# Rotation pieces, half buffers, small clears and a norm's scaled sum in a two-layer diffusion step

## The chip, the cores and the metric

The kernel runs on one core of a Trainium2 chip. The metric is the device time of one launch in microseconds; the median of the runs is compared. TensorE does the matrix products, VectorE (DVE in the rows) and ScalarE (ACT) the elementwise work, GpSimd (POOL) elementwise work and its own DMA queue, and SyncE (SP) issues most loads.

## The reference, cut to what matters

One inference step of a backbone of width 1024 over 128 context and 512 latent tokens (640 in all), two layers. Layer 0 is attention: queries and keys are normed per head,

```
q = rms_norm(qkv[:, :, 0], q_gain); k = rms_norm(qkv[:, :, 1], k_gain)
rms_norm(x, g) = x * rsqrt(mean(x * x) + EPS) * g
```

context tokens attend to one another, latent tokens to a two-dimensional neighbourhood and to 256 cached context keys. Layer 1 is a diagonal complex state-space mixer in two directions: 64 groups of 16 channels, 64 states each, `x[t] = a x[t-1] + B u[t]`, `y = Re(C x) + D u`, then GELU and a gated linear map. Each layer is followed by a SwiGLU FFN of width 2816; every part begins with an RMS norm, modulated by a shift and a scale that come from the conditioning.

## The kernel before, in words

Activations lie with features on the partitions and the 640 tokens along the free dimension, in two halves of 320. A float32 product is made of three products of rounded parts: a matrix is split into a high part (ScalarE copies it) and a low part (VectorE or Pool subtracts).

The stages in order are `attention_layer`, `attention_out`, `ffn`, `ssm_layer`, `glu` and `fast_ffn`. TensorE's order in attention is written out by hand; on the other engines a planner that simulates the timeline orders the instructions, by program order and its own estimate of when each is ready. `issue_after` holds instructions back until a given one has been placed.

**Attention.** `start` norms the input and projects queries and keys of the first pair of heads. `projections` does the other eleven jobs (seven of queries and keys, four of values); each job has three groups of token tiles (two, two and one). A group of queries and keys goes through `qk_norm`: ScalarE squares, VectorE sums per head (L578), Pool forms the mean plus epsilon (L580) and its power of -0.5 (L581), VectorE scales (L588, tile `yn`). Eight steps later `qk_store` transposes the result on TensorE (L606, tile `tq`). A group of values goes through `v_split`. Between those steps run 80 attention units (`scores`, `weigh`, `values`), one for each pair of heads, query block and head.

**Rotations.** The state-space layer needs tables of powers of a complex number (`rotations`, one call for each of eight feature tiles). Pool computes them in the background of attention: doublings by L1180 to L1182, copies by L1189 to L1193 and a store to memory. `rotations` is a generator of nine pieces for each tile, 72 in all, that `self.turns` yields. `qk_norm` takes two or three pieces each time, and the loop of units one piece for each of the last 32 units (L405). In `start` the list is empty.

**Preparation of the state-space matrices.** `ssm_prep` is a generator too, taken step by step within `attention_out` and `ffn`. After its first part it goes through 16 steps (a feature tile and a half of it). A step loads the next step's chunk (`cb`, two buffers) and inputs (`qb`, two buffers), forms the chunk outputs (`co`, one buffer, stored to `cd`), then by a complex product `cmul` the input matrices (`bout`, one buffer for real and imaginary part, stored to `bd`), then the chunk response (`td` in memory, copied to `md`). All these loads and stores go through Pool's queue.

**State-space layer.** `ssm_tables` loads the tables of one feature tile; that of tile 0 is called within `ffn`. `states` calls it for the others and loads the response matrix `mt` by itself. Before the loop Pool clears `xb` (5200 columns) and both `w` (657 columns each). `ssm_input`, just before, norms the FFN's output into `u`, sends it to `uu` through SP's and Pool's queues, and takes the sums of squares of the last feature tiles.

Of the kernel before, what the change touches and what calls it, by code (L numbers as in the profile page):

```python
# [11 lines left out]
F32 = mybir.dt.float32  # L12
# [5 lines left out]
ALU = mybir.AluOpType  # L18
# [4 lines left out]
P = 128  # L23
D = 1024
KT = D // P
# [3 lines left out]
HEADS = 16  # L29
HD = 64  # L30
# [4 lines left out]
EPS = 1e-6  # L35
# [3 lines left out]
GC = 16  # L39
TC = 8  # L40
GT = P // GC
NST = 64
NCOL = 81
WROW = 82
# [55 lines left out]
class Kernel:  # L100
# [240 lines left out]
    def attention_layer(self, x0):  # L341
        tc, nc, a = self.tc, self.nc, self.a
        with ExitStack() as es:
# [10 lines left out]
                jobs += [("qk", 2 * c), ("v", c), ("qk", 2 * c + 1)]  # L354
            self.jobs = iter(jobs)
            self.jw, self.jqk, self.jv = [], {}, {}
            self.turns = iter(())
            with tc.manual_schedule(engines={nc.tensor.engine}):
                self.start(x0, es)
            ot = self.xp.tile([P, NPAIR, NTOK], F32, tag="x", name="ot")  # L360
            fill = itertools.chain(self.projections(len(jobs) - 1), self.out_start(ot))
            ada = iter([(wh, ft) for wh in (GA, 4, 3) for ft in range(KT)])
            self.ed = self.dp.tile([KT, P, 2, GT, NCOL], F32, name="ed")
            self.turns = itertools.chain(*(self.rotations(ct) for ct in range(KT)))
            units = [(hp, b, j) for hp in range(NPAIR) for b in range(-1, 4) for j in range(2)]
            n = len(units)

# [5 lines left out]
            with tc.manual_schedule(engines={nc.tensor.engine}):  # L373
                while at < PRE - JOB:
                    next(fill)
                    at += 1
                    if at == -JOB + FA:
                        self.qk_store(self.first[0][0], 0, 2, 0)
                    if at == -JOB + FB:
                        for t, y in enumerate(self.first[1]):  # L380
                            self.qk_store(y, 2 + 2 * t, 2 - t, 0)
                for i in range(-4, n + 1):
                    to = (PRE - JOB) * (-1 - i) // 4 if i < 0 else goal[min(i + 1, len(goal) - 1)]
                    if i + 4 < n:
                        st[i + 4] = self.scores(*units[i + 4])
                    half = at + (to - at) // 2
                    while at < half:
                        next(fill, None)
                        at += 1
                    if 0 <= i + 2 < n:  # L390
                        self.weigh(st[i + 2])
                    if i > 0 and units[i - 1][2]:
                        self.turn(st[i - 1], ot)
                        if i % 10 == 0:
                            self.turned.append(i // 10 - 1)
                    while at < to:
                        next(fill, None)
                        at += 1
                    if 0 <= i < n:
                        self.values(st[i], st.get(i - 1))  # L400
                    if i >= 0 and i % 10 in (3,6,9):
                        w = next(ada, None)
                        if w:
                            self.later(*w, 0)
                    if i >= n - 2 * HEADS:  # L405
                        next(self.turns, None)
                for _ in fill:
                    pass
                for _ in self.turns:
                    pass  # L410
                self.out_split(ot)
# [155 lines left out]
    def qk_norm(self, parts):  # L567

        nc = self.nc
        v = lambda ap: ap.rearrange("p (t d) -> p t d", d=HD)  # L570
        ss = self.ap.tile([P, 12], F32, tag="ss", name="ss", bufs=4)
        sums, g = [], 0
        for ps in parts:
            n = ps.shape[1]
# [2 lines left out]
            sums.append(ss[:, g : g + n // HD])  # L577
            nc.vector.tensor_reduce(sums[-1], v(sq), axis=AX.X, op=ALU.add)  # L578
            g += n // HD
        nc.gpsimd.tensor_scalar(ss[:, :g], ss[:, :g], 1.0 / HD, EPS, op0=ALU.mult, op1=ALU.add)  # L580
        last = nc.gpsimd.tensor_tensor(ss[:, :g], ss[:, :g], self.mhalf[:, :g], op=ALU.pow)  # L581
        ys, c = [], 512
        for ps, r in zip(parts, sums):
# [5 lines left out]
            c += n  # L589

        with self.tc.issue_after(last.ins):
            for _ in range(2 if n > 256 else 3):
                next(self.turns, None)
        return ys

# [28 lines left out]

    def v_split(self, c, ps, t0, n):
        nc = self.nc
        if t0 == 0:
            y = self.ap.tile([P, 2 * P], F32, tag="rr", name="vnew")
            nc.scalar.activation(y, ps[:, 0].rearrange("p h d -> p (h d)"), AF.Copy)
            nc.sync.dma_start(self.o["new_v"][:, c * 2 * P : (c + 1) * 2 * P], y)  # L630
        for pr in range(2):
            vp = self.jv[2 * c + pr]
            self.v_parts(lambda i: vp[:, i, t0 : t0 + n, :], ps[:, :, pr, :])
# [454 lines left out]
    def ssm_prep(self):  # L1088
# [56 lines left out]
        steps = [(ct, h) for ct in range(KT) for h in range(2)]  # L1145
        cb, qb, copies, before = self.load_chunk(0, 0), self.load_inputs(0, 0, qd), [], None
        for n, (ct, h) in enumerate(steps):
            ahead = n + 1 < len(steps) and (self.load_chunk(*steps[n + 1]), self.load_inputs(*steps[n + 1], qd))
            c = self.chunk_outputs(ct, h, pt, fe, cb)
            yield  # L1150
            self.input_matrices(ct, h, qb)
            cb, qb = ahead or (None, None)
            yield
            if copies:
                copies.pop()()
            if before:
                copies.append(self.chunk_response(*before, dcol))
                yield
            before = ct, h, c
        copies.pop()()  # L1160
        self.chunk_response(*before, dcol)()

    def rotations(self, ct):

# [42 lines left out]
    def input_matrices(self, ct, h, qb):  # L1207

        nc, sp = self.nc, self.sp
        n = 8 * NST  # L1210
        o = sp.tile([P, 2, n], F32, tag="o", name="bout")
        tmp = sp.tile([P, n], F32, tag="tmp", name="btmp")
        self.cmul(nc.vector, o[:, 0, :], o[:, 1, :], qb[:, 0, 0, :], qb[:, 0, 1, :], qb[:, 1, 0, :], qb[:, 1, 1, :], tmp)
        nc.gpsimd.dma_start(self.bd[ct, :, :, 4 * h : 4 * h + 4, :].rearrange("p i g l -> p i (g l)"), o)

    def load_chunk(self, ct, h):

        cb = self.sp.tile([P, 2, 2, 4, GC], F32, tag="cb", name="cb", bufs=2)
        self.nc.gpsimd.dma_start(cb.rearrange("p a i g c -> p (a i g c)"), self.a["ssm_cb"][2 * ct + h])
        return cb  # L1220

# [35 lines left out]
    def chunk_response(self, ct, h, c, dcol):  # L1257
# [7 lines left out]
            dm[64:], self.ident[64:MR, 64:MR].unsqueeze(1).broadcast_to([GC, n, GC]),  # L1265
            dcol[64:, gs : gs + n].unsqueeze(2).broadcast_to([GC, n, GC]), op=ALU.mult,
        )
        td = self.dp.tile([GC, n, (2 * TC - 1) * GC], F32, tag="td", name="td", bufs=2)
        kk = sp.tile([MR, n, LS * GC], F32, tag="kk", name="kk")
        ps = self.aux.tile([P, 512], F32, tag="aux", name="kkps")  # L1270
        with self.tc.issue_after(self.done.ins), self.tc.high_priority(offset=-LOW):
# [46 lines left out]
    def ssm_tables(self, ct):  # L1318
# [6 lines left out]
        cm = [(self.mp if ct % 2 else self.tables).tile([P, 2, GT // 2, P], F32, tag="cm", name="cm", bufs=2) for _ in range(2)]  # L1325
        for h in range(2):
            nc.sync.dma_start(cm[h], self.cd[ct, h])
        return bt, et, cm

    def ssm_layer(self):  # L1330
        tc, nc, a = self.tc, self.nc, self.a
# [4 lines left out]
        with self.ssm as es:  # L1336
# [13 lines left out]
            nc.gpsimd.memset(dmask[:, LC + 1 : LC + 2], 0.0)  # L1350
            w = [rp.tile([P, NW + 1], F32, name=f"w{i}") for i in range(2)]
            xb = rp.tile([P, 8 * NX + 16], F32, name="xb")
            nc.gpsimd.memset(xb, 0.0)
            dc = rp.tile([P, NW + 1], F32, name="dec")
            nc.gpsimd.memset(dc[:, NW:], 0.0)
            for i in range(2):
                nc.gpsimd.memset(w[i], 0.0)
            self.z, zt = self.htiles(True)
            def states(ct):

                tab = self.tab.pop(ct) if ct in self.tab else self.ssm_tables(ct)
                mt = [mp.tile([P, GT // 2, P], F32, tag="mt", name="mt", bufs=3) for _ in range(2)]
                for h in range(2):
                    self.loaded = nc.sync.dma_start(mt[h], self.md[ct, h])
                ps = []
                for i in range(2):
                    s = psa.tile([P, 2, 512], F32, tag=f"s{i}", name="sps")
# [241 lines left out]
```

## Time and profile before

| | |
|---|---|
| median of 3 runs | 1746.0 us (1740.94 to 1749.78) |
| profiled execution, its own time | 1747.1 us |
| its span | 1745.3 us |
| TensorE, weight loads | 1628.6 us (93%), 1564.8 us (90%) |
| VectorE | 1358.8 us (78%) |
| ScalarE | 698.7 us (40%) |
| Pool | 569.7 us (33%) |
| mean granted TensorE clock | 0.961 |

The span runs from the first to the last instruction of one profiled execution. Busy time of an engine leaves out its waits; an engine that is 93% busy has little left to give, but an average hides stretches in which it waits or runs at a lower granted clock. Attention ends near 440 us, the output map near 500, the first FFN near 1030, the state-space layer near 1180.

### The profile page before, as it was taken

To read this page: it belongs to the slowest core of one execution; us is meant where nothing else is said; L and a number is where in the kernel's file an instruction comes from. 1 tells how busy PE (TensorE), PEld (TensorE's weight loads), DVE (VectorE), ACT (ScalarE), POOL (GpSimd) and SP (SyncE) were. 2 spreads that over 40 slices of the span, in tenths; PEclk is the share of its full clock that TensorE was granted. 3 is DMA by queue.
4 is the path that set the end of the run, shared out by engine and by line. 5 is a ranking of instruction groups with operands and counts; after the bars stand their busy time and mean duration, and the time that the engine had idled before them with its cause. 6 is when DMAs were issued, how large, how long until landed. Compare 5 with 4: busy or idle time off the path is not lost.

```text
span 1745.3 us, 31855 instructions
## 1 busy us (share of the span) xinstructions
PE 1628.6 (93%) x12172; PEld 1564.8 (90%) x12172; DVE 1358.8 (78%) x2812; ACT 698.7 (40%) x1616; POOL 569.7 (33%) x848
## 2 busy tenths in 40 slices
PE   7999999988989989998899967989999899999999
PEld 1899899877979989998799967979999899999999
DVE  7677778786897778977896667986789975994793
ACT  4555555564554221322322233333245432551450
POOL 1155454976411322332230012240005612531430
PEclk9899999996999989999899987989999999999999
DMA  9233323343445676777677317856421131222222
GB/s 356 78 103 107 125 100 117 103 137 109 118 118 171 191 203 187 229 205 187 182 218 256 108 33 195 252 157 223 155 97 49 67 103 59 87 97 73 73 80 79
DMA packets 93369, 243.86 MB, mean 140 GB/s; under 512 B 24544, under 2 KB 34336, under 8 KB 92064
## 3 DMA queue, kind: packets, MB, share of 16 engines
q1 hardware_dynamic: 71520, 194.02, 34.0%
q0 software_dynamic: 21696, 47.80, 10.7%
q8 instruction: 96, 1.57, 0.4%
q14 instruction: 57, 0.47, 0.1%
HBM read 209.04 MB, written 31.52 MB: 138 GB/s over the span
## 4 chain that ended last, share of the span: by engine, by line
PE 68%; DVE 18%; DMA 6%; issue 3%; POOL 3%; ACT 2%; SPq 0%; DVEq 0%; POOLq 0%; ACTq 0%
PE p L166 27%; PE qkps L530 8%; PE fz L914 3%; PE pg L166 3%; PE pv L166 3%; DMA bd<-bout 3%; PE mmps L166 3%; DVE adaj L198 2%; PE po L706 2%; PE fy L914 2%; PE s L668 2%; PE fx L914 2%; PE fv L914 2%; PE fw L914 2%; PE s L670 2%
## 5 line engine op out<-in xcount | busy, mean ns | idle before, releaser
L166 PE MATMUL p<-bt,wh 128*128 128x320 f32 x1408 | 322.3, 316 | 13.8 <-DVE silu L814 7.4
L166 PEld LDWEIGHTS p<-bt,wh 128*128 128x128 f32 x1408 | 241.0, 192 | 16.6 <-DVE bt L241 6.7
L166 PE MATMUL p<-hh,wh 128*128 128x320 f32 x704 | 221.9, 316 | 13.1 <-ACT hh L244 12.3
L166 PE MATMUL p<-hh,wl 128*128 128x320 f32 x704 | 221.4, 315 | 4.6 <-DVE wl L114 4.6
L166 PE MATMUL p<-bt,wl 128*128 128x320 f32 x704 | 221.2, 315 | 0.8 <-DVE wl L114 0.7
L166 PE MATMUL p<-hl,wh 128*128 128x320 f32 x704 | 221.3, 315 | 0.7 <-DVE hl L245 0.7
L198 DVE SCALAR_TENSOR_TENSOR adaj<-adaw,cs 128x1024 bf16<-128x1024 f32 x160 | 197.1, 1232 | 0.3
L909 POOL TENSOR_TENSOR wsum<-wraw 128x512 f32<-128x512 f32 x90 | 125.9, 1400 | 206.3 <-DVE wl L245 145.0
L530 PE MATMUL qkps<-wh,hh 128*128 128x256 f32 x480 | 152.5, 318 | 0.0
L166 PEld LDWEIGHTS p<-hh,wh 128*128 128x128 f32 x704 | 134.7, 191 | 14.3 <-ACT hh L244 13.1
L113 ACT ACTIVATE wh<-wraw 128x1024 fp32r<-128x1024 f32 (+1 forms) x100 | 103.9, 1040 | 100.5 <-DMA wraw<-in_w 48.1
L166 PEld LDWEIGHTS p<-hh,wl 128*128 128x128 f32 x704 | 134.7, 191 | 5.1 <-DVE wl L114 5.1
L114 DVE TENSOR_TENSOR wl<-wraw,wh 128x1024 fp32r<-128x1024 f32 (+1 forms) x98 | 120.2, 1228 | 23.9 <-ACT wh L113 22.9
L530 PE MATMUL qkps<-wh,hl 128*128 128x256 f32 x480 | 137.5, 286 | 0.8 <-DVE hl L241 0.8
L530 PE MATMUL qkps<-wl,hh 128*128 128x256 f32 x480 | 137.4, 286 | 0.0
L166 PEld LDWEIGHTS p<-bt,wl 128*128 128x128 f32 x704 | 134.8, 192 | 1.4 <-DVE wl L114 1.4
L166 PEld LDWEIGHTS p<-hl,wh 128*128 128x128 f32 x704 | 134.4, 191 | 1.5 <-DVE hl L245 1.3
L245 DVE TENSOR_TENSOR wl<-wraw,wh 128x512 fp32r<-128x512 f32 (+1 forms) x128 | 103.2, 815 | 28.2 <-ACT wh L244 28.0
L251 DVE SCALAR_TENSOR_TENSOR ot<-p,mod,ot 128x64 f32<-128x64 f32 x192 | 64.5, 381 | 67.2 <-PE p L166 67.1
L244 ACT ACTIVATE wh<-wraw 128x512 fp32r<-128x512 f32 (+1 forms) x128 | 76.1, 611 | 83.1 <-PE p L166 57.3
L245 DVE TENSOR_TENSOR wl<-wsum,wh 128x512 fp32r<-128x512 f32 x90 | 92.7, 1030 | 15.0 <-ACT wh L244 14.5
L530 PEld LDWEIGHTS qkps<-wh,hh 128*128 128x128 f32 x480 | 93.0, 194 | 9.5 <-issue 1.5
(381 smaller groups left out, 4450.5 us busy)
## 6 DMA issues: line engine op xcount, KB each, us to landing
adaw<-in_ada SPq DMA_DIRECT2D x80, 512.0 KB, 3.9
wraw<-in_w SPq DMA_DIRECT2D x60, 512.0 KB, 4.6
wraw<-in_w SPq DMA_DIRECT2D x30, 1024.0 KB, 5.0
wraw<-in_w_qk SPq DMA_DIRECT2D x16, 512.0 KB, 3.8
qb<-in_ssm_bc POOLq DMA_DIRECT2D x16, 512.0 KB, 10.1
qb<-qd POOLq DMA_DIRECT2D x16, 512.0 KB, 8.4
cd<-co POOLq DMA_DIRECT2D x16, 512.0 KB, 8.4
bd<-bout POOLq DMA_DIRECT2D x16, 512.0 KB, 11.1
```

What stands on the lines that cost most here:

```text
L113: nc.scalar.activation(wh[:, :nk, :], raw[:, :nk, :], AF.Copy)
L114: (eng or nc.vector).tensor_tensor(wl[:, :nk, :], raw[:, :nk, :], wh[:, :nk, :], op=ALU.subtract)
L166: self.done = self.nc.tensor.matmul(ps, w[x][k // 4][:, k % 4, :] if isinstance(w[x], list) else w[x][:, k, :], h[y][k][:, c0 : c0 + HALF] ...
L198: nc.vector.scalar_tensor_tensor(junk, raw, 1.0, self.cs[:, cond, :], op0=ALU.mult, op1=ALU.mult, accum_out=self.macc[:, layer, which, ft, ...
L244: self.nc.scalar.activation(hi, x, AF.Copy)
L245: self.mark = self.nc.vector.tensor_tensor(lo, x, hi, op=ALU.subtract)
L251: self.mark = nc.vector.scalar_tensor_tensor(xi, pi, self.modcol(layer, gate_which, m, c), xi, op0=ALU.mult, op1=ALU.add)
L530: self.nc.tensor.matmul(ps, self.h[x][k][:, t * P : (t + 1) * P], w[y][k // 4][:, k % 4, :], start=(k == 0 and i == 0), stop=(k == KT - 1 ...
L668: nc.tensor.matmul(s[:, PAST:], qk[x][rows, 0, qc : qc + P], c[y][rows, :], start=(i == 0), stop=(i == 2))
L670: nc.tensor.matmul(s[:, :n], qk[x][rows, 0, qc : qc + P], qk[y][rows, 1, kc : kc + n], start=(i == 0), stop=(i == 2))
L909: nc.gpsimd.tensor_tensor(v, q[:, x], q[:, y], op=op)
L914: nc.tensor.matmul(ps[n], w[x][:, k * P : (k + 1) * P], b[right][y][:, k, :], start=(k == 0 and i == 0), stop=(k == 3 and i == 2))
```

## The change

- `self.ed` and `self.turns` are made before `start`, so that its two norms take pieces too. Every norm takes two pieces, every `v_split` takes two (with nothing that holds them back), and the loop of units none.
- In `qk_norm` the scaled sum is formed by VectorE; the power stays on Pool.
- In `ssm_prep` the next chunk is loaded after the present chunk's outputs are formed, into one buffer in place of two. `input_matrices` writes real and imaginary part to tiles of half the size, with three buffers, and stores each by a DMA of its own. The response's tile in memory has three buffers in place of two, and its copy to `md` is issued a step later.
- `ssm_tables` loads `mt` too, from a pool that is open during the FFN.
- Of `xb` only the first 16 columns of rows 1 to 7 and the last 16 are cleared, of each `w` only nine columns.

```diff
@@ attention_layer
+            self.ed = self.dp.tile([KT, P, 2, GT, NCOL], F32, name="ed")
+            self.turns = itertools.chain(*(self.rotations(ct) for ct in range(KT)))
-            self.turns = iter(())
             with tc.manual_schedule(engines={nc.tensor.engine}):
                 self.start(x0, es)
...
-            self.ed = self.dp.tile([KT, P, 2, GT, NCOL], F32, name="ed")
-            self.turns = itertools.chain(*(self.rotations(ct) for ct in range(KT)))
...
-                    if i >= n - 2 * HEADS:
-                        next(self.turns, None)
@@ qk_norm
-        nc.gpsimd.tensor_scalar(ss[:, :g], ss[:, :g], 1.0 / HD, EPS, op0=ALU.mult, op1=ALU.add)
+        nc.vector.tensor_scalar(ss[:, :g], ss[:, :g], 1.0 / HD, EPS, op0=ALU.mult, op1=ALU.add)
         last = nc.gpsimd.tensor_tensor(ss[:, :g], ss[:, :g], self.mhalf[:, :g], op=ALU.pow)
...
         with self.tc.issue_after(last.ins):
-            for _ in range(2 if n > 256 else 3):
+            for _ in range(2):
                 next(self.turns, None)
@@ v_split
+        for _ in range(2):
+            next(self.turns, None)
@@ ssm_prep
-            ahead = n + 1 < len(steps) and (self.load_chunk(*steps[n + 1]), self.load_inputs(*steps[n + 1], qd))
+            more = n + 1 < len(steps)
+            ahead = self.load_inputs(*steps[n + 1], qd) if more else None
             c = self.chunk_outputs(ct, h, pt, fe, cb)
+            cb = self.load_chunk(*steps[n + 1]) if more else None
             yield
             self.input_matrices(ct, h, qb)
-            cb, qb = ahead or (None, None)
+            qb = ahead
             yield
-            if copies:
-                copies.pop()()
+            if len(copies) > 1:
+                copies.pop(0)()
...
-        copies.pop()()
-        self.chunk_response(*before, dcol)()
+        copies.append(self.chunk_response(*before, dcol))
+        for c in copies:
+            c()
@@ input_matrices
-        o = sp.tile([P, 2, n], F32, tag="o", name="bout")
+        o = [sp.tile([P, n], F32, tag="o", name="bout", bufs=3) for _ in range(2)]
...
-        nc.gpsimd.dma_start(self.bd[ct, :, :, 4 * h : 4 * h + 4, :].rearrange("p i g l -> p i (g l)"), o)
+        for i in range(2):
+            nc.gpsimd.dma_start(self.bd[ct, :, i, 4 * h : 4 * h + 4, :].rearrange("p g l -> p (g l)"), o[i])
@@ load_chunk
-        cb = self.sp.tile([P, 2, 2, 4, GC], F32, tag="cb", name="cb", bufs=2)
+        cb = self.sp.tile([P, 2, 2, 4, GC], F32, tag="cb", name="cb")
@@ chunk_response
-        td = self.dp.tile([GC, n, (2 * TC - 1) * GC], F32, tag="td", name="td", bufs=2)
+        td = self.dp.tile([GC, n, (2 * TC - 1) * GC], F32, tag="td", name="td", bufs=3)
@@ ssm_tables
-        return bt, et, cm
+        mt = [self.tables.tile([P, GT // 2, P], F32, tag="mt", name="mt", bufs=3) for _ in range(2)]
+        for h in range(2):
+            self.loaded = nc.sync.dma_start(mt[h], self.md[ct, h])
+        return bt, et, cm, mt
@@ ssm_layer
-            nc.gpsimd.memset(xb, 0.0)
+            nc.gpsimd.memset(xb[:, NX : 8 * NX].rearrange("p (r c) -> p r c", c=NX)[:, :, :16], 0.0)
+            nc.gpsimd.memset(xb[:, 8 * NX :], 0.0)
...
-                nc.gpsimd.memset(w[i], 0.0)
+                nc.gpsimd.memset(w[i][:, 0 : NW + 1 : WROW], 0.0)
...
-                tab = self.tab.pop(ct) if ct in self.tab else self.ssm_tables(ct)
-                mt = [mp.tile([P, GT // 2, P], F32, tag="mt", name="mt", bufs=3) for _ in range(2)]
-                for h in range(2):
-                    self.loaded = nc.sync.dma_start(mt[h], self.md[ct, h])
+                *tab, mt = self.tab.pop(ct) if ct in self.tab else self.ssm_tables(ct)
```

## Rows read from the trace of the kernel before

**Rows 1.** The page: busy us, share of the span, instructions.

```profile
PE 1628.6 (93%) x12172; PEld 1564.8 (90%) x12172; DVE 1358.8 (78%) x2812; ACT 698.7 (40%) x1616; POOL 569.7 (33%) x848
```

**Rows 2.** Busy time by stretch: its length, engines, granted clock, DMA share, GB/s.

```profile
core 0: us, PE busy (x) PEld busy (x) DVE busy (x) ACT busy (x) POOL busy (x), PEclk, DMA share, GB/s
70.00:92.00 22.00, 22.00 (x95) 19.76 (x96) 11.58 (x33) 10.34 (x26) 0.00 (x0) 0.53 0.14 49
380.00:400.00 20.00, 8.04 (x70) 7.00 (x69) 12.51 (x24) 9.85 (x21) 19.19 (x25) 0.62 0.67 217
400.00:420.00 20.00, 19.50 (x138) 16.95 (x136) 13.13 (x35) 8.11 (x26) 18.44 (x49) 0.53 0.31 104
520.00:870.00 350.00, 323.43 (x2177) 320.58 (x2178) 276.22 (x546) 106.50 (x208) 97.64 (x139) 0.95 0.70 196
```

**Rows 3.** Waits of TensorE, 60 to 440 us: total, times, longest.

```profile
PE tq L606 <- DVE yn L588: 23.4, 11, 6.1
```

**Rows 4.** Timeline of Pool in attention: start, duration, instruction.

```profile
381.33 0.65 POOL L580 TENSOR_SCALAR ss<-ss 128x8 f32<-128x8 f32 x1
382.06 2.04 POOL L732 TENSOR_TENSOR hl<-ot,hh 128x640 fp32r<-128x640 f32 x1
...
386.21 1.64 POOL L581 TENSOR_TENSOR ss<-ss,mhalf 128x8 f32<-128x8 f32 x1
```

**Rows 5.** Timeline of TensorE there; in brackets the idle time before.

```profile
388.64 1.11 PE L606 MATMUL tq<-ident,yn 128*128 128x128 f32 x4 [6.11 <-DVE yn L588]
...
398.75 0.66 PE L606 MATMUL tq<-ident,yn 128*128 128x128 f32 x2 [5.85 <-DVE yn L588]
```

**Rows 6.** Waits of TensorE, 520 to 870 us.

```profile
PE p L166 <- ACT hh L244: 10.4, 2, 5.9
PE p L166 <- DVE silu L814: 7.4, 2, 4.8
```

**Rows 7.** Waits of VectorE, 500 to 870 us.

```profile
DVE bout L1014 <- DMA bd<-bout: 56.8, 12, 6.7
...
DVE co L1014 <- DMA cd<-co: 2.7, 2, 1.6
```

**Rows 8.** Timeline of Pool in one step of the preparation: its issues.

```profile
608.72 0.62 POOL L1204 DMA_DIRECT2D qb<-in_ssm_bc  x1
609.31 0.76 POOL L1214 DMA_DIRECT2D bd<-bout  x1
616.35 0.88 POOL L1234 DMA_DIRECT2D cd<-co  x1 [6.28 <-DVE co L1022]
```

**Rows 9.** Timeline of VectorE in that step.

```profile
605.29 0.68 DVE L1016 TENSOR_TENSOR bout<-bout,btmp 128x512 f32<-128x512 f32 x1
...
623.14 0.69 DVE L1014 TENSOR_TENSOR bout<-qb 128x512 f32<-128x512 f32 x1 [6.67 <-DMA bd<-bout]
...
629.53 0.76 DVE L1014 TENSOR_TENSOR co<-ptab,cb 128x576 f32<-128x576 f32 x1
```

**Rows 10.** DMA issues by line: count, size, median us to landing.

```profile
cd<-co POOLq DMA_DIRECT2D x16, 512.0 KB, 8.4
bd<-bout POOLq DMA_DIRECT2D x16, 512.0 KB, 11.1
...
md<-td POOLq DMA_DIRECT2D x16, 256.0 KB, 3.5
```

**Rows 11.** Timeline of Pool before the state-space layer.

```profile
1031.49 4.47 POOL L1353 MEMSET xb<- 128x5200 f32 x1 [8.31 <-PE p L166]
```

**Rows 12.** Timeline of VectorE there (rows of equal form merged).

```profile
1029.84 0.63 DVE L1310 TENSOR_SCALAR u<-xr,mod 128x64 f32<-128x64 f32 x2
...
1031.38 4.76 DVE L1310 TENSOR_SCALAR u<-xr,mod 128x64 f32<-128x64 f32 x2
```

**Rows 13.** One line's instructions: duration ns, min/median/max.

```profile
L580 POOL TENSOR_SCALAR ss<-ss x23: 192/197/1056, 59.1 to 394.9; 128x8 f32<-128x8 f32 x15, 128x4 f32<-128x4 f32 x7, 128x12 f32<-128x12 f32 x1
```

**Rows 14.** VectorE's groups, 60 to 440 us: busy us, mean ns, idle before.

```profile
L210 DVE TENSOR_SCALAR mod<-macc,adab 128x2 f32<-128x2 f32 x16 | 5.1, 316 | 0.0
```

**Rows 15.** Waits of TensorE, 1020 to 1180 us.

```profile
PE y L1414 <- DMA mt<-md: 2.6, 1, 2.6
```

More of the change, by code (lines that the diff above doesn't have):

```diff
@@ L1210, in input_matrices @@
         n = 8 * NST
-        o = sp.tile([P, 2, n], F32, tag="o", name="bout")
+        o = [sp.tile([P, n], F32, tag="o", name="bout", bufs=3) for _ in range(2)]
         tmp = sp.tile([P, n], F32, tag="tmp", name="btmp")
-        self.cmul(nc.vector, o[:, 0, :], o[:, 1, :], qb[:, 0, 0, :], qb[:, 0, 1, :], qb[:, 1, 0, :], qb[:, 1, 1, :], tmp)
-        nc.gpsimd.dma_start(self.bd[ct, :, :, 4 * h : 4 * h + 4, :].rearrange("p i g l -> p i (g l)"), o)
+        self.cmul(nc.vector, *o, qb[:, 0, 0, :], qb[:, 0, 1, :], qb[:, 1, 0, :], qb[:, 1, 1, :], tmp)
+        for i in range(2):
+            nc.gpsimd.dma_start(self.bd[ct, :, i, 4 * h : 4 * h + 4, :].rearrange("p g l -> p (g l)"), o[i])
     def load_chunk(self, ct, h):
-        cb = self.sp.tile([P, 2, 2, 4, GC], F32, tag="cb", name="cb", bufs=2)
+        cb = self.sp.tile([P, 2, 2, 4, GC], F32, tag="cb", name="cb")
         self.nc.gpsimd.dma_start(cb.rearrange("p a i g c -> p (a i g c)"), self.a["ssm_cb"][2 * ct + h])
```

## The prediction

> **What bounds the kernel now.** The page comes first: TensorE is busy 1628.6 us of 1745.3 [rows 1], so about 117 us of its idle time, and whatever it runs at half clock, is all that edits on the other engines can give back. The stretches show where that lies [rows 2]. From 70 to 92 us the granted clock is 0.53 while Pool does nothing; from 380 to 420 it is 0.62 and 0.53 while Pool is busy 37.6 of 40 us, and from 380 to 400 TensorE works only 8.0 of 20 us; from 520 to 870 us TensorE lacks 26.6 of 350 us and the clock is 0.95. The two levels are 1.2 and 2.4 GHz, so a mean of 0.95 means a tenth of the stretch at the lower one.
>
> Then I ask which wait ends last in each stretch. In attention it is the transposes of normed queries and keys: 23.4 us in 11 waits [rows 3]. Pool's timeline shows why the largest is there [rows 4]: the scaled sum runs at 381.33, then the split of an output tile (2.04 us) and two rotation instructions come, and the root only at 386.21. Between sum and root the planner fitted other ready Pool work. TensorE waits 6.11 us for this norm and 5.85 us for the next [rows 5].
>
> In the first FFN TensorE waits for the gate's halves and products, which VectorE forms or feeds: 10.4 and 7.4 us [rows 6]. VectorE itself stands still 56.8 us in 12 waits for the write of the previous input matrix [rows 7]. One step shows it [rows 8, 9]: the write goes out at 609.31, just behind the loads of the next step (the second of them at 608.72), and VectorE, which wants to overwrite the buffer, is held 6.67 us, to 623.14. Such a write lands after 11.1 us, a chunk output after 8.4, a response copy of half the size after 3.5 (medians) [rows 10].
>
> Before the SSM layer Pool clears a tile for 4.47 us from 1031.49 [rows 11]. In the same microseconds two VectorE instructions that took 0.63 us at 1029.84 take 4.76 us [rows 12].
>
> **The change part by part.** The sum is made against the profiled execution: 1747.1 us beside a span of 1745.3; the median of the runs shown is 1.1 us lower.
>
> *Scaled sum on VectorE.* Pool loses 23 instructions with a median of 0.197 us [rows 13]; VectorE gains 23. The nearest VectorE row, a scalar operation on two columns, has 0.316 us [rows 14]: 7.3 us more work for VectorE, behind which its splits and reductions queue. It had 12.5 of 20 us busy from 380 to 400 [rows 2], so I cost it at nothing; without that cover it is 7.3 us. What counts is the pair: no foreign work can stand between sum and root. At 381.33 that was 4.9 us, less the new instruction. The Trainium skill (GPSIMD Engine Reference, section 4.1, Engine selection) says that an operation with one input runs about as fast on GpSimd as on VectorE. The rows make VectorE's the longer by 0.12 us, 2.7 us over 23; by the rule that is nothing, by the rows it is hidden anyway.
>
> *Rotation pieces.* There are 72 (nine for each of eight tiles). Before, 49 follow norms and the last 23 are drawn in the last 32 attention units, which is why Pool is full from 380 to 420 [rows 2]. After, four follow the two norms of the start, 42 the other 21 norms, 24 the twelve splits of values; two are left over. Every Pool instruction of a piece counts, the store of each tile's table too, but their number is the same. So Pool should be nearly free at the last norms, and work where it stood idle: 0.00 us from 70 to 92 [rows 2]. The two largest waits, 11.96 us [rows 5], I let shrink to 3 us, as one output split (2.04 us) may still come first: -9. The other nine waits hold 11.4 us, a good part of it not Pool's; I take -3. Bounds for both: 0 and -23.4.
>
> The clock from 380 to 420: the lower level holds 34 us ((1-0.62) x 2 x 20 and (1-0.53) x 2 x 20). At full speed TensorE's 19.5 us there could halve, but VectorE is busy 13.1 of the second 20 us [rows 2], so at most 6.9 us can go there, and about 2 before 400: bounds 0 and -9, taken -6, if the shorter waits keep the clock up.
>
> At the start the second norm's root now has two pieces ahead of it, where Pool was idle before. Nearest price: nothing but the pair's 0.2 us gained, or the 4.9 us of [rows 4]. The pieces' instructions are short and the root can go in between: +1.
>
> *Half buffers.* Three buffers of half a matrix take the place of one whole one: a product's real half may overwrite what was sent two steps ago, and its imaginary half the previous real half. That one was ready at 605.97 (605.29 plus 0.68 [rows 9]), before the loads went out, so its write need not run behind them. The 12 waits of 56.8 us go. What is late next is the chunk output, which keeps its one buffer: sent at 616.35, landed 8.4 us later at about 624.8, and overwritten from 629.53 [rows 8, 10]. In this step 4.8 of the 6.67 us can come forward; in two steps VectorE already waits for that landing (2.7 us [rows 7]) and nothing can. I take half. TensorE's 26.6 us idle [rows 2], less some 3 us of other causes, give half of 23.6, -12. The clock: a tenth of 350 us is 35 us at the lower level; TensorE loses half of what it works in it, between 4 us (if all idle time lies in it) and 17.5 (if none); half of the middle, -5.5. Bounds of the whole: -2 and -26.6-17.5 = -44.
> Sixteen more writes cost Pool some 0.75 us each, as the one at 609.31 does [rows 8], 12 us over 350 in which it is busy 98 [rows 2]; what queues behind are the loads and stores above, so nothing, or 12 us if all were on the path. The chunk's loads move from a step ahead to the end of the step before, on Pool's queue, ahead of the write; they are small and I cost them at nothing, as a whole step lies before their use; at the worst VectorE waits where it waited for the write. The third response buffer and the later copies only take a wait out of Pool's queue.
>
> *Small clears.* The clear falls from 5200 columns to 128, and the two VectorE instructions should return to 0.63 us: -4.1, on the path, since the last sums of squares queue behind them on VectorE. Bounds: 0, if the norm finds another wait, and -4.5. The response matrix of the first tile is loaded during the FFN; TensorE's 2.6 us wait for it [rows 15] goes, but VectorE is the later there: 0, at best -2.6.
>
> **Sum:** -9 -3 -6 +1 -12 -5.5 -4.1 = -38.6; 1747.1 - 38.6 - 1.1 = 1707 us.
>
> **The rivals.** *All of it comes back:* both kinds of wait vanish and the clock stays up: -23.4 -9 -26.6 -11 -4.1 -2.6 +1 = -76, about 1670 us. For it: single causes with many waits; against: the chunk output's one buffer, and waits that are not Pool's. 0.20.
>
> *The chunk output takes over the wait:* VectorE stands as long, one buffer later, and the FFN gives 3 us instead of 17.5: 1722 us. For it: the waits already there [rows 7]. 0.22. The Trainium skill (DMA: Bandwidth & Descriptors, Anatomy of one DMA, SWDGE path) gives each such transfer a fixed part of about 2 us; by it 16 more transfers put 32 us into the queue ahead of the chunk output's landing, an estimate that would eat the FFN's whole gain: 1725 us. The rows have 3.5 us for 256 KB and 11.1 for 512 [rows 10], which speaks for no such loss.
>
> *Slower:* the pieces set free by value splits wait for no norm, so six can pile up before the first root of the next job, after each of four value jobs, and at the start. Price of such a place: 4.9 us [rows 4] and a low clock as from 70 to 92 (0.47 x 22 = 10 us [rows 2]), 15 us. It decides from three places on, when it cancels the gain; with four, 1747.1 - 1.1 - 38.6 + 60 = 1767 us. Against it: queries and keys with two or three pieces a norm ran well from 92 to 380. 0.06.
>
> *It doesn't do what it says:* the planner, which orders Pool and VectorE by its own estimate, puts other work ahead of the root all the same, and the FFN's gain goes to the chunk output; the clear alone remains: about 1742 us. 0.06.
>
> **How the numbers follow.** My forecast, 1707 us, has 0.46. Half a per cent (8.7 us) is about what this kernel's measurement can tell. Faster by more: 0.46 + 0.20 + 0.22 = 0.88; same 0.06; slower 0.06. The range leaves out the last two and the lower part of the first rival (some 0.08): 1676 to 1735.
>
> **What would show it.** Right: the transposes' waits fall below 10 us in all with none above 3; Pool's root follows VectorE's scalar operation directly; Pool is mostly idle from 400 us on; no wait of the matrix product for its write, a new wait of the chunk output for its own; the two VectorE instructions near 0.6 us. Wrong: a low clock after a value job, with rotation pieces ahead of a root; VectorE's idle time in the FFN as large as before; a gain made up elsewhere by another order of the planner.

## The result, and the profile after

The changed kernel takes 1720.3 us (median of 4 runs, 1714.31 to 1725.56) where the kernel before takes 1746.7 beside it: a ratio of 0.9857, 95% interval 0.9826 to 0.9887. By the ratio that is 25 us less (20 to 30), faster as forecast and inside the range, but two thirds of the 38.6 us of the sum. A second series gave 0.9832 (0.9803 to 0.9861).

The profiled execution's span fell from 1745.3 to 1722.2 us. Three marks on TensorE divide it:

| stretch | before | after | won | forecast |
|---|---|---|---|---|
| start to the output map's first product into `p` | 493.1 | 484.1 | 9.0 | 17 |
| from there to the state-space layer's first sum of squares | 528.9 | 518.9 | 10.0 | 17.5 |
| from there to the first product of `glu` | 160.8 | 156.5 | 4.3 | 4.1 |
| the rest | 562.5 | 562.7 | -0.2 | 0 |

The page's line of busy times, and the stretches of [rows 2] with that of the table's second row (columns as there):

```profile
span 1722.2 us, 31861 instructions
...
PE 1621.3 (94%) x12172; PEld 1560.4 (91%) x12172; DVE 1357.4 (79%) x2835; ACT 699.7 (41%) x1616; POOL 562.5 (33%) x842
```

```profile
70.00:92.00 22.00, 21.27 (x103) 19.06 (x104) 13.04 (x36) 11.23 (x29) 13.87 (x37) 0.61 0.22 75
380.00:400.00 20.00, 14.57 (x139) 12.82 (x140) 14.45 (x35) 9.21 (x29) 17.05 (x23) 0.55 0.65 233
400.00:420.00 20.00, 20.00 (x154) 17.82 (x154) 12.97 (x34) 9.52 (x27) 0.00 (x0) 0.68 0.14 44
520.00:870.00 350.00, 328.92 (x2267) 327.31 (x2266) 297.52 (x587) 108.45 (x209) 109.79 (x162) 0.97 0.75 207
484.10:1003.00 518.90, 491.89 (x3373) 488.27 (x3373) 414.58 (x837) 160.58 (x309) 128.13 (x195) 0.97 0.66 187
```

Pool now works from 70 to 92 us and is empty from 400 on, as expected. But from 380 to 400 it is still busy 17.05 us, and the clock there is 0.55: with the 0.68 behind it the lower level holds 18 + 12.8 = 31 of the 40 us, where it held 34 before. In the FFN's stretch, the table's second row, TensorE's idle time fell from 31.0 to 27.0 us and its busy time from 497.9 to 491.9. Its waits from 520 to 870 us answer to [rows 6]; the longest are now 7.9 and 7.3 us:

```profile
PE p L166 <- DVE hl L245: 15.2, 2, 7.9
PE p L166 <- ACT hh L244: 5.7, 4, 3.3
```

TensorE's waits in attention answer to [rows 3]; the second line has the end of its last wait under another name:

```profile
PE tq L603 <- DVE yn L585: 8.9, 6, 2.6
PE tq L603 <- DVE sm L680: 5.1, 2, 4.8
```

23.4 us have become 14.0. The two largest, 11.96 us [rows 5], are 2.64 and 4.76:

```profile
380.46 0.66 PE L603 MATMUL tq<-ident,yn 128*128 128x128 f32 x4 [2.64 <-DVE yn L585]
...
388.47 0.66 PE L603 MATMUL tq<-ident,yn 128*128 128x128 f32 x2 [4.76 <-DVE sm L680]
```

For the second of them, VectorE forms the scaled sum at 384.54, and Pool takes the root at 386.85; between them Pool ends a split and runs three rotation instructions:

```profile
384.54 1.03 DVE L577 TENSOR_SCALAR ss<-ss 128x4 f32<-128x4 f32 x1
...
385.51 0.41 POOL L1183 TENSOR_TENSOR etmp<-powers 128x128 f32<-128x128 f32 x1
385.88 0.62 POOL L1182 TENSOR_TENSOR powers<-powers 128x256 f32<-128x256 f32 x1
386.46 0.43 POOL L1184 TENSOR_TENSOR powers<-powers,etmp 128x128 f32<-128x128 f32 x1
386.85 1.02 POOL L578 TENSOR_TENSOR ss<-ss,mhalf 128x4 f32<-128x4 f32 x1
```

VectorE's waits in the FFN (500 to 870 us) answer to [rows 7]:

```profile
DVE bout L1013 <- DMA bd<-bout: 40.8, 13, 5.9
DVE co L1013 <- DMA cb<-in_ssm_cb: 8.5, 7, 2.5
```

This is the row that the prediction did not have: the wait of the product for its write, which the half buffers should end, is still there, 40.8 us after 56.8. A wait of the chunk output for its own write, the rival's sign, is not there at all. One step of VectorE, and Pool's issues in it, show how (compare [rows 8, 9]):

```profile
617.35 0.68 DVE L1021 TENSOR_TENSOR bout<-bout,btmp 128x512 f32<-128x512 f32 x1
...
620.75 0.69 DVE L1016 TENSOR_TENSOR bout<-qb 128x512 f32<-128x512 f32 x1
...
625.36 0.75 DVE L1021 TENSOR_TENSOR co<-co,ctmp 128x576 f32<-128x576 f32 x1
631.48 0.69 DVE L1013 TENSOR_TENSOR bout<-qb 128x512 f32<-128x512 f32 x1 [5.36 <-DMA bd<-bout]
```

```profile
616.42 0.55 POOL L1217 DMA_DIRECT2D bd<-bout  x1 [2.00 <-DVE silu L813]
618.57 0.72 POOL L1292 DMA_DIRECT2D md<-td  x1 [1.60 <-DMA td<-kk]
619.28 0.63 POOL L1205 DMA_DIRECT2D qb<-qd  x1
619.89 0.61 POOL L1206 DMA_DIRECT2D qb<-in_ssm_bc  x1
620.49 0.60 POOL L1217 DMA_DIRECT2D bd<-bout  x1
```

The real half goes out at 616.42, ahead of the loads; the imaginary half, finished at 618.03, behind them at 620.49, and it lands 11 us later. The multiplication that is held until 631.48 begins a real half (L1013). Between L1021, which ends a product at 617.35, and this L1013 stands the L1016 of the next product, but not yet its L1015; so the L1013 belongs to the product after the next. With three buffers its real half overwrites the imaginary half just sent. VectorE waits for a write that its next product does not need.

### The profile page after: what moved, and what is told of

Same layout as the page of the kernel before. It is cut to its first block, busy times and chain, and to the rows that moved or that the text cites. A ratio compares the mean times of both kernels' runs of the same rounds, so it can differ in the third digit from the quotient of the medians.

```text
span 1722.2 us, 31861 instructions
## 1 busy us (share of the span) xinstructions
PE 1621.3 (94%) x12172; PEld 1560.4 (91%) x12172; DVE 1357.4 (79%) x2835; ACT 699.7 (41%) x1616; POOL 562.5 (33%) x842
## 3 DMA queue, kind: packets, MB, share of 16 engines
q8 instruction: 96, 1.57, 0.4%
## 4 chain that ended last, share of the span: by engine, by line
PE 73%; DVE 11%; DMA 5%; issue 4%; POOL 3%; ACT 2%; SPq 1%; DVEq 0%; ACTq 0%; POOLq 0%
PE p L166 31%; PE qkps L527 9%; PE fz L913 3%; PE pg L166 3%; PE pv L166 3%; PE mmps L166 3%; PE po L705 2%; PE s L667 2%; DMA bd<-bout 2%; PE fx L913 2%; PE s L669 2%; PE fv L913 2%; PE fw L913 2%; PE fy L913 2%; PE y L1422 2%
## 5 line engine op out<-in xcount | busy, mean ns | idle before, releaser
L166 PE MATMUL p<-bt,wh 128*128 128x320 f32 x1408 | 317.3, 312 | 5.9 <-DVE bt L241 5.0
```

The costliest lines, as they stand in the source:

```text
L166: self.done = self.nc.tensor.matmul(ps, w[x][k // 4][:, k % 4, :] if isinstance(w[x], list) else w[x][:, k, :], h[y][k][:, c0 : c0 + HALF] ...
```

## The experiments

The interval of a ratio is some 5 us to either side, so differences under 5 us are read from traces alone. One trace is not finer than that either. Over the fourteen profiles of this document (before, changed twice, and the variants below) the table's stretches take:

| stretch | | us |
|---|---|---|
| first | old attention (3 profiles) | 486.8 to 493.1 |
| | new attention (10; the late pieces apart, 493.4) | 470.7 to 484.1 |
| second | chunk loaded early (4) | 527.1 to 533.0 |
| | chunk loaded later, products not held (8) | 516.7 to 526.4 |
| | products in order (2) | 488.3 and 488.5 |
| third | whole clears (3) | 158.9 to 160.9 |
| | small clears (11) | 153.7 to 162.6 |

The ranges of the first stretch do not overlap, those of the second only just do not, and those of the third do: its 4.3 us are within the spread.

**Each part alone.** The kernel before with only the edits to `attention_layer`, `qk_norm` and `v_split`; with only those to the preparation; with only the small clears. The earlier load of `mt` is in none of the three.

> The kernel before with the rotation pieces and the scaled sum alone. If the stages add up, as the two traces aligned instruction by instruction suggest (9.5 us won by the end of attention, 9.5 more by the end of the first FFN, 4 more before the state-space layer), the time falls by about 9.5 us, to 1737 us, and the waits for the normed queries and keys show 14 us in all, as in the changed kernel. If instead the attention part also sets free something later (Pool, the queues), it falls by more than 13 us; if the FFN gives it back because its waits depend on the phase, by less than 5 us.

> The kernel before with the edits to the preparation of the state-space matrices alone (half buffers, one chunk buffer, third response buffer). If the early product is what keeps VectorE waiting, the waits of the product for its write stay at 35 to 45 us and the time falls by about 9.5 us, to 1737 us. If the remaining wait of the changed kernel comes from a collision with the other edits, the waits fall below 20 us here and the time by 15 us or more.

> The kernel before with the small clears alone, without the earlier load of the response matrix. By the prediction's term the wait of the sums of squares falls from 6.4 to about 2.3 us and the time by 4 us, to 1742 us. By the rival that the next waits take it back (the first products of the state-space layer wait for the normed input on its way through the queue) it falls by 2 us at most.

Measured: 0.9957 (0.9931 to 0.9984), 0.9934 (0.9905 to 0.9963) and 0.9999 (0.9973 to 1.0025), so 7.5, 11.5 and 0 us less. In the first the transposes' waits are 14.1 us in the two rows; in the second the product's waits for its write 43.3. The parts, 19 us together, agree with the 25 of the whole within their intervals, and what holds VectorE in the FFN comes with the preparation's edits, not from a collision. The clears, in TensorE's waits from 1000 to 1180 us:

```profile
PE sps L1371 <- DMA uu<-u: 12.7, 1, 12.7
...
PE ms L228 <- DVE acc L225: 2.3, 1, 2.3
```

The sums of squares wait 2.3 us where the kernel before shows 6.4, but the next wait, for the input's way through the queue, is 12.7 us where it was 10.5. The stretch to `glu` is 155.5 us after 160.8, a difference within the spread above, and the runs show none: 4 us are just inside the interval, and the rival of at most 2 us is the likelier.

**The scaled sum back on Pool.**

```diff
-        nc.vector.tensor_scalar(ss[:, :g], ss[:, :g], 1.0 / HD, EPS, ...)
+        nc.gpsimd.tensor_scalar(ss[:, :g], ss[:, :g], 1.0 / HD, EPS, ...)
```

> The changed kernel with the scaled sum back on Pool, all else as changed. If the pair of sum and root kept apart was a cause of its own, the waits for the normed queries and keys rise again by 4 us or more and the time by 4 to 10 us, to 1725 to 1730 us. If the rotation pieces alone had put the foreign work there, nothing changes within 3 us. If VectorE's own queue ahead of the sum costs more than the split pair did, it is faster than the changed kernel, by 2 to 5 us.

Measured: 0.9855 (0.9812 to 0.9899), the changed kernel's own ratio. The transposes wait 14.5 us in all, the two largest 2.64 and 5.59 us. Forming the sum on VectorE is worth nothing that the time shows.

**Products in order.** Each product's first multiplication is placed behind the last addition of the product before, which `cmul` now returns:

```diff
+        with ExitStack() as es:
+            if self.product:
+                es.enter_context(self.tc.issue_after(self.product.ins))
-        self.cmul(nc.vector, *o, ...)
+            self.product = self.cmul(nc.vector, *o, ...)
```

Beside it the same chip ran the changed kernel again, and two more variants: the next inputs' loads issued behind the product's writes, and (below) the output splits behind the last norm. The edit for the loads:

```diff
-            ahead = self.load_inputs(*steps[n + 1], qd) if more else None
...
             self.input_matrices(ct, h, qb)
-            qb = ahead
+            if more:
+                with self.tc.issue_after(self.sent.ins):
+                    qb = self.load_inputs(*steps[n + 1], qd)
```

> The changed kernel once more, beside the three that follow and on the same chip, so that they can be set against it: 1.4% under the kernel before, as in its first runs, with waits of the input matrices' product for its write near 41 us. Both theories expect the same of it.

> The changed kernel; a product's first multiplication is placed on VectorE behind the last addition of the product before it, and nothing else is changed. If the planner's early placing is what holds VectorE (the multiplication stands almost a whole step ahead and waits for the imaginary half's write, which runs behind two loads), the 40.8 us of waits for the write fall below 10 us, the two long waits of TensorE in the FFN (7.9 and 7.3 us) go, and the time falls by 10 to 18 us against the changed kernel. If the buffers or the queue are simply short and the place makes no difference, the waits move to the next instruction (loads, chunk) and the time stays within 4 us.

> The changed kernel with the next inputs' loads issued behind the writes of the product, on the same queue. If it is the order on the queue that delays the imaginary half's write, it lands after about 4 us in place of 9 to 12, and the waits for the write fall below 10 us; but the same multiplication also needs the loads, which now land later, so by the theory of the early place VectorE waits for them instead, and most of the 40 us stay: the gain is 0 to 8 us. If the write's place on the queue is the whole cause, the gain is 10 to 18 us as with the products in order.

Measured: changed again 1721.2 us (0.9832); in order **1690.8 us**, 0.9655 (0.9628 to 0.9683); loads behind writes 1723.1, 0.9852 (0.9825 to 0.9879). The order in which VectorE's instructions stand in the built program of the changed kernel, and then of the one in order (place, line, what it waits for; SW are counters of Pool's queue; lines between them are left out):

```
1073 L1021 TENSOR_TENSOR bout<-bout,btmp 128x512 [waits DVE_49]
1074 L1016 TENSOR_TENSOR bout<-qb 128x512 [waits DMASW3_49]
1084 L1013 TENSOR_TENSOR bout<-qb 128x512 [waits DMASW6_49,DMASW5_49,DMASW4_49]
1089 L1014 TENSOR_TENSOR btmp<-qb 128x512 [waits DVE_49]
1090 L1015 TENSOR_TENSOR bout<-bout,btmp 128x512 [waits DVE_49]
...
1069 L1021 TENSOR_TENSOR bout<-bout,btmp 128x512 [waits DVE_49]
1071 L1013 TENSOR_TENSOR bout<-qb 128x512 [waits DMASW6_49,DMASW5_49,DMASW0_49]
1074 L1016 TENSOR_TENSOR bout<-qb 128x512 [waits DMASW3_49]
```

In the first list L1013 stands ahead of L1014 and L1015 of the product before it; in the second it does not. With that alone VectorE has no wait for `bd` left, and TensorE works without a gap from 520 to 870 us:

```profile
520.00:870.00 350.00, 350.00 (x2487) 350.00 (x2486) 313.29 (x620) 109.29 (x209) 117.26 (x173) 1.00 0.82 233
```

The FFN's stretch of the table is 488.3 us where it was 518.9: 30.6 us, 21.1 of them idle time and 9.5 busy time at the lower clock. My 10 to 18 us had left out the clock, and the idle time alone is more. With the loads behind the writes VectorE waits as long, for the loads:

```profile
DVE bout L1013 <- DMA qb<-in_ssm_bc: 57.0, 12, 7.1
```

So the order on the queue is not the cause: the instruction placed a step early waits for whichever transfer comes last.

**Which edit won the FFN's 10 us.** One whole buffer again in place of the halves; then also the two chunk buffers with their early load, which leaves only the later copies of the response and their third buffer:

```diff
-        o = [sp.tile([P, n], F32, tag="o", name="bout", bufs=3) for _ in range(2)]
+        o = sp.tile([P, 2, n], F32, tag="o", name="bout")
...
-            ahead = self.load_inputs(*steps[n + 1], qd) if more else None
+            ahead = n + 1 < len(steps) and (self.load_chunk(*steps[n + 1]), self.load_inputs(*steps[n + 1], qd))
...
-            cb = self.load_chunk(*steps[n + 1]) if more else None
...
-        cb = self.sp.tile([P, 2, 2, 4, GC], F32, tag="cb", name="cb")
+        cb = self.sp.tile([P, 2, 2, 4, GC], F32, tag="cb", name="cb", bufs=2)
```

> The changed kernel with one whole buffer for the input matrices in place of three halves, one write in place of two; the single chunk buffer, the later copies, attention and clears stay as changed. With one buffer the products cannot run ahead of one another, and VectorE's order is the same with or without the hold of the run with the products in order. If the half buffers as such gave the changed kernel its gain in the first FFN (about 10 us), the waits for the write return to 55 us or more and the time rises by 5 to 12 us against the changed kernel. If the gain came from the other edits there (the chunk's load, the third response buffer), it stays within 4 us. Either way it stands some 30 to 40 us above the run with the products in order, if that one needs both the half buffers and the order.

> The changed kernel with the whole buffer for the input matrices and also the two chunk buffers and their early load of the kernel before; of the edits to the preparation only the third response buffer and the later copies are left. The stretch from the output map's first matmul to the state-space layer's first sum of squares took 528.9 us in the kernel before, 518.9 in the changed one and 519.3 with the whole buffer alone. If the later copies are what shortened it (Pool no longer holds its queue for a response that has not landed), it stays near 519 us and the time near 1716. If the chunk's later load into one buffer is the cause, it returns to about 529 us and the time rises by 8 to 10 us, to 1725.

Measured: 1715.5 us, 0.9823 (0.9785 to 0.9861), and 1729.7 us, 0.9909 (0.9874 to 0.9944). The stretch is 519.3 us with the whole buffer and 527.1 with the early chunk, against 518.9 and 528.9. VectorE's waits, first of the one and then of the other:

```profile
DVE bout L1013 <- DMA bd<-bout: 36.6, 10, 6.5
DVE bout L1013 <- DMA td<-kk: 10.4, 2, 5.4
```

```profile
DVE bout L1013 <- DMA bd<-bout: 58.4, 13, 6.9
DVE bout L1013 <- DMA td<-kk: 6.7, 1, 6.7
```

The half buffers, as the change has them, win nothing; the later copies next to nothing. The chunk's later load into one buffer wins the stretch's 8 to 10 us: the intervals of these two runs lie apart, and so do the ranges of the table above, both narrowly. How it does so was not taken apart. One row bears on it: the chunk output's write, 8.4 us to landing before [rows 10] and 7.6 with the early chunk, lands after 5.0 with the later load, in the changed kernel and with the whole buffer alike:

```profile
cd<-co POOLq DMA_DIRECT2D x16, 512.0 KB, 5.0
```

Of the two outcomes expected of the whole buffer, a loss of 5 to 12 us and none within 4, the second came. The products in order with one whole buffer were not run; that the 30 us need the half buffers too is argued from the 36.6 us that VectorE waits for the one buffer's write, and not shown.

**The end of attention.** The output splits placed behind the last norm's square, root and scaling; and, in another run, the value splits' 24 pieces moved back to the last 32 units (`v_split` draws none, the loop of units one each, as before).

```diff
         for k in self.turned[:n]:
+            with ExitStack() as es:
+                for i in (self.turnstile, self.root, self.normed):
+                    es.enter_context(self.tc.issue_after(i.ins))
...
```

> The changed kernel; the splits of the attention output for the output map are placed behind the last norm's square on ScalarE, its root on Pool and its scaling on VectorE. If the two waits left at the end of attention (2.6 and 4.7 us) come from these splits on all three engines, they fall to 1 us each or less, the low clock of the 20 us behind them goes or shortens, and the time falls by 5 to 15 us. If the waits come from the root's own chain (square, sum, root, scaling: about 4 us from row to row) whatever stands between, they stay above 2 us each and the time within 4 us, or it rises because the splits are then late for the output map.

> The changed kernel with the 24 pieces of the value splits drawn one for each of the last 32 units, as in the kernel before; the scaled sum stays on VectorE. If a full Pool at the last norms was what cost the kernel before its two largest waits, Pool is again busy over 35 of the 40 us at the end of attention, the two waits rise from 7 to 11 us or more, and the time by 4 to 10 us. If the waits there belong to the whole burst of work on ScalarE and VectorE, they and the time stay within 3 us of the changed kernel.

Measured: 0.9851 (0.9824 to 0.9879), as the changed kernel; and 0.9943 (0.9917 to 0.9969), some 15 us slower. With the splits held back the norms' two waits fall to 1.65 and 0.78 us, but six copies and a weight's copy run on ScalarE ahead of the softmax, and TensorE waits for that:

```profile
375.65 0.74 ACT L733 ACTIVATE hh<-ot 128x640 fp32r<-128x640 f32 x1
...
378.78 0.73 ACT L244 ACTIVATE hh<-ot 128x640 fp32r<-128x640 f32 x1
379.41 1.05 ACT L113 ACTIVATE wh<-wraw 128x1024 fp32r<-128x1024 f32 x1
380.35 0.68 ACT L679 ACTIVATE p<-s,sm 128x512 f32<-128x512 f32 x1
```

```profile
376.86 0.66 PE L603 MATMUL tq<-ident,yn 128*128 128x128 f32 x4 [1.65 <-DVE yn L585]
...
381.18 1.11 PE L688 MATMUL pt<-ident,p 128*128 128x128 f32 x4 [2.60 <-ACT p L679]
...
383.28 0.69 PE L603 MATMUL tq<-ident,yn 128*128 128x128 f32 x2 [0.78 <-ACT ot L725]
```

The wait moves; with the 2.78 us for VectorE's part of the softmax at 384 it is as long. With the late pieces Pool is full again:

```profile
380.00:400.00 20.00, 13.54 (x121) 12.05 (x117) 17.53 (x35) 12.37 (x30) 18.69 (x26) 0.66 0.64 217
400.00:420.00 20.00, 20.00 (x166) 17.61 (x165) 12.52 (x35) 9.25 (x30) 18.26 (x52) 0.66 0.30 104
```

But the two waits at the end are 3.30 and 3.15 us, together less than in the changed kernel, so a full Pool alone does not make them. The time goes elsewhere. Beside the second profile of the changed kernel, whose clock was as high at the start, the last product of `values` comes 13.7 us later (433.1 and 419.3), lost at waits and low clocks between 147 and 372 us, and 6 us more at the output map, where TensorE waits 5.8 us for a normed input. The chain that ended last runs there through a load of weights of 12.9 us, up to 491.8; what makes the other losses was not followed.

**Products in order, and the splits held behind the softmax weights of their unit**, so that they come one by one (`ph` and `pl` are the copies of the weights in `weigh`):

```diff
-                for i in (self.turnstile, self.root, self.normed):
+                for i in (self.turnstile, self.root, self.normed, self.ph, self.pl):
```

> The kernel with the products in order; the splits of the attention output are placed behind the softmax weights of the unit where they stand in the program as well, so that they no longer come in one burst. If that burst is what keeps TensorE waiting at the last norms, the waits of the queries and keys at the end of attention and the waits of the softmax together fall from some 10 us to below 4, the clock stays up from 380 to 400, and the time falls by 5 to 12 us against 1691. If the output map then waits for its input instead, the time stays within 4 us and a new wait of the map for its split shows.

Measured: 1684.4 us, 0.9636 (0.9601 to 0.9670), against 0.9655 (0.9628 to 0.9683) with the products in order alone: the intervals overlap, and the gain of 3 to 6 us is not shown by the runs. The trace bears the mechanism out in part: the two norms' waits are 1.65 and 2.12 us, and the clock around them is 0.87 where it is 0.62 with the products in order alone, so that 10 of these 40 us lie at the lower level and not 30; in exchange the output map's first products wait 3 us for their splits. First the products in order alone, then with the splits spread:

```profile
370.00:410.00 40.00, 32.60 (x261) 28.81 (x262) 27.60 (x66) 19.29 (x54) 19.03 (x25) 0.62 0.44 147
370.00:410.00 40.00, 32.75 (x329) 28.31 (x329) 33.59 (x78) 23.03 (x64) 20.94 (x26) 0.87 0.51 164
```

Both are faster than the changed kernel, by some 30 us or more.

## Why the prediction was right, and where its steps were not

**Direction and range held; the likeliest time was 13 us too low,** and the time stands at the rival's 1722 us without the rival's mechanism. That the range held is in part luck: some 10 of the 25 us come from an edit that the prediction costed at nothing, and most of its signs of being right did not come: the transposes' waits are 14.0 us with one of 4.76, the root does not follow the sum directly at the largest wait, the product still waits for its write, and the chunk output does not wait for its own.

**Half buffers, -17.5: the step that failed.** The prediction followed the buffers rightly (a real half overwrites what was sent two steps ago) and then took VectorE's order for given. The half buffers let the planner place the first multiplication of a product a whole step earlier, and there it waits for the imaginary half, behind two loads, as the whole matrix did before. Against one whole buffer the halves are worth nothing; the 10 us of the stretch come with the chunk's later load into one buffer, which I had costed at nothing. With the order held, the same buffers give 30.6 us in the stretch (26.6 and 17.5 of idle time and clock were my upper bounds, 44 together).

**Chunk output as the next wait.** It did not come: no such wait in the changed kernel, where the chunk output's write lands after 5.0 us and not the 8.4 of the sum. With the products in order VectorE waits for weights and chunk loads, none of which TensorE feels. Sixteen more writes show no cost either. The estimate from the Trainium skill (DMA: Bandwidth & Descriptors, Anatomy of one DMA, SWDGE path) of 32 us on the queue does not come out as a cost: the run in order has the same 32 writes, and TensorE is busy 350.0 of 350 us.

**Two largest root waits, -9: measured -4.6.** "One output split may still come first" was too few: square, sum and root each met splits on their engine. Nor did the sum on VectorE keep foreign work from between sum and root, as the prediction has it, for Pool ran three rotation instructions there and was busy 17.05 of the 20 us where it should have been nearly free. Removing the splits from there moves the wait to the softmax.

**Clock from 380 to 420, -6: about nothing.** With waits of 2.64 and 4.76 us left there, 31 of the 40 us still lie at the lower level; in the second profile of the changed kernel, where the same waits come some 8 us earlier, 27 us from 360 to 410 (clock 0.73).

**The other waits, -3: measured -4.8** (from 11.4 to 6.6 us). **Scaled sum:** costed at nothing for VectorE, rightly (0.161 us each, Pool's had 0.197), but credited with keeping the pair together. With the sum on VectorE alone at the end of attention (late pieces) the two waits are 6.45 us, with the pieces moved and the sum on Pool 8.23, with both 7.40, with neither 11.96: in these single profiles either does, and beside the moved pieces the sum's place changes no time. The Trainium skill's rule (GPSIMD Engine Reference, section 4.1, Engine selection) that an operation with one input runs at roughly line rate on GpSimd too fits 0.161 us on the one engine and 0.197 on the other, though four to twelve columns are too few to test a rate.

**Small clears, -4.1: right for the wait, not shown in the time.** The two instructions take 0.63 us again, and the wait for the sums of squares falls from 6.4 to 2.3 us:

```profile
1015.12 0.63 DVE L1313 TENSOR_SCALAR u<-xr,mod 128x64 f32<-128x64 f32 x2
```

The wait for `mt` went as well, but the wait for `uu` took 2.3 us back (12.8 after 10.5), and the clears alone change no time.

**Pieces piling up after value splits (slower):** no sign of it; with those pieces moved to the end the kernel is slower.

## What to carry to other kernels

A buffer that is added to end a wait also frees the scheduler to run ahead: look where the waiting instruction will stand in its engine's queue, not only at what it must wait for. If it moves a step forward, hold it behind the instruction after which it is due, and price the buffer and the order together. Work taken from one engine in a burst that three engines share moves the wait to the next consumer; spread it before expecting the clock back.

## What the runs showed of the hardware

The granted clock at one place differs between executions of one program. From 70 to 92 us the changed kernel had 0.61 in the one profile and 1.00 in the other, and its last product of `values` came at 429.6 and 419.3 us; the preparation alone, which leaves attention as it was, had 1.00 where [rows 2] has 0.53. First the second profile of the changed kernel, then the preparation alone:

```profile
70.00:92.00 22.00, 20.28 (x157) 18.22 (x156) 18.62 (x49) 15.18 (x40) 17.63 (x40) 1.00 0.26 91
```

```profile
70.00:92.00 22.00, 22.00 (x187) 20.13 (x186) 17.98 (x52) 15.74 (x42) 0.00 (x0) 1.00 0.20 61
```

So ten microseconds of one attention profile need not come from an edit, and the 9.0 us of the table's first row are to be read beside the 7.5 of the part alone.

Elementwise instructions of VectorE and Pool can stretch when they run at the same time. The clear of 5200 columns on Pool is the plain case: the two VectorE instructions beside it took 4.76 us [rows 11, 12], and 0.63 with the small clear. At the end of attention the same split took 1.57 and 2.59 us on Pool, and the last scaled sum, which began at 384.54 while Pool's 2.59 us ran, 1.03 us on VectorE against a median of 0.161; that the one made the other is not shown there:

```profile
375.34 1.57 POOL L731 TENSOR_TENSOR hl<-ot,hh 128x640 fp32r<-128x640 f32 x1 [6.17 <-ACT hh L730]
...
382.95 2.59 POOL L731 TENSOR_TENSOR hl<-ot,hh 128x640 fp32r<-128x640 f32 x1
```

```profile
L577 DVE TENSOR_SCALAR ss<-ss x23: 151/161/1033, 59.9 to 384.5; 128x8 f32<-128x8 f32 x15, 128x4 f32<-128x4 f32 x7, 128x12 f32<-128x12 f32 x1
```
